# A list scheduler told other durations, and the Delta stage's projections in another order

## The chip, the core and the metric

The kernel runs on one core of one Trainium2 chip. Four engines do the work: TensorE (PE in the profile) multiplies, VectorE (DVE), ScalarE (ACT) and GpSimd (POOL) do the element-wise rest; SyncE (SP) issues most of the DMA. Each engine takes its instructions in the order in which the program lists them. The time is the device time of one execution in microseconds, the median of three runs. Before the change it is 1763.18 us (1761.16 to 1765.25).

## What is computed

512 tokens of width 1024 go through a block of two layers and then through a second block. A layer is a mixer and a gated feed-forward part, each with norms around it. The first layer's mixer is a dilated attention, the second layer's a gated delta rule in both directions ("Delta stage" here); both have an attention over a memory of 256 rows beside them. The mixer that the change touches, cut down:

```python
def _deltanet_sublayer(h, mem_n, w_in, conv_w, a_log, dt_bias, out_norm, w_out, w_mem_kv):
    qkv, z, gate_in, q_mem = jnp.split(h @ w_in, [...], axis=-1)
    qkv = lax.conv_general_dilated(qkv, conv_w[:, None, :], ...)
    q, k, v = jnp.split(jax.nn.silu(qkv), 3, axis=-1)       # six heads of 128
    q = _l2norm(q.reshape(b, s, DN_HEADS, DN_HEAD_DIM)) * (DN_HEAD_DIM ** -0.5)
    k = _l2norm(k.reshape(b, s, DN_HEADS, DN_HEAD_DIM))
    ...
    o = _gated_delta_chunked(q, k, v, ...) + rev(_gated_delta_chunked(rev(q), rev(k), ...))
    o = o * lax.rsqrt(jnp.mean(o * o, axis=-1, keepdims=True) + EPS) * out_norm * jax.nn.silu(zf)
    mem_out = _memory_attention(q_mem, mem_n, w_mem_kv)
    return jnp.concatenate([o, mem_out], axis=-1) @ w_out

def _gated_delta_chunked(q, k, v, g, beta):                  # chunks of 64 tokens
    ...
    sol = lax.linalg.triangular_solve(a, rhs, lower=True, unit_diagonal=True)
    u, w = sol[..., :dv], sol[..., dv:]
    def step(state, inp):
        v_new = uc - w @ state
        out = (q * exp(g)) @ state + intra @ v_new
        state = state * exp(g_last) + k.T @ v_new
        return state, out
```

The first block's second half, the norms and the second block's mixers are computed as well; the change leaves their arithmetic alone.

## The kernel before

**Precision.** A wide product is made of three matmuls: both operands are split into a high and a low part, and `mm3` (lines 271 to 273) issues low times high, high times low and high times high into one bank of PSUM. A weight arrives by DMA as `raw`, ScalarE writes its high part `wh` (line 243), VectorE or GpSimd its low part `wl` (line 262). A projection of 128 columns is eight such products of 128x512, over eight tiles of the width.

**Stages.** To about 75 us: norms of memory and tokens, the memory's keys and values, biases. To about 235 us: dilated attention and the memory's attention. To about 660: out-projection and feed-forward part of the first layer (`out_ffn`, line 1022). To about 1006: the Delta stage (`deltanet`, line 1170). To about 1430: its out-projection and the second feed-forward part. Then the second block, to 1756.

**What sets the order.** The whole program is laid out when the kernel is built, by a list scheduler, class `Flow`. Every piece of work is a generator that yields an engine and a stated duration and then emits its instructions; `run` (line 105 on) keeps a modelled time for each engine, and takes, of all pieces that are ready, the one that can start first in that model, with ties inside 0.1 us settled by a number `late`. A hand-over from one engine to another counts `HOP` = 0.2. The stated durations are those of `act`, `dve` and `pool` (lines 149 to 160) and the numbers in the yields: 0.33 for a product of 256 columns, 0.65 for one of 512. So a stated duration changes no instruction; it changes where each instruction stands in its engine's order, everywhere behind it.

**The Delta stage.** `deltanet_weights` (line 1161) gives the order in which the 27 projections of the stage run: `g` for the gates, four kinds `k`, `q`, `v`, `z` (`z` is the output gate) for each of six heads, and two `m`, the memory's queries. For each head, the triangular solve is an inverse by doubling: products `x` (lines 1519 and 1523), then `y` (1544), copies of `U` on VectorE (1548) and of `xT` on ScalarE (1530), at the end `y` (1566) and `Uf` (1571, on VectorE; 1558 on GpSimd). Then four steps of a chain, forward and backward side by side: product with `Uf` (1602), `vn` on ScalarE (1605), `vs` on VectorE (1610), product (1612), state `St` on VectorE (1616, 1619), product (1594), `rhs` on VectorE (1597), and again; the output `o` is made beside it (1624, 1625). `gate_out` (1645) then takes the head's row sums, the norm (GpSimd, 1352 and 1658), the transposition `poT` (1335) and the gate (1661); 1706 and 1708 split the result into `Xh` and `Xl` for the out-projection. The memory's attention (`mem_attention`, line 842) has the products `ms_s` (858), `ms_t` (882) and `mo` (898).

**What fills the waits.** Projections, products of the memory's attention and of other heads stand between the steps of a head. Once all projections are through, the out-projection of the stage may begin: `OUT[1]` (line 1727) lets a first group of three token tiles run over the tiles of the width in the order 6, 7, 0, 1, 2, 3, 4, 5, so that 21 products (those over the first seven) need nothing of the last head.

Of the kernel before, what the change touches and what calls it, by code (L numbers as in the profile page):

```python
# [35 lines left out]
S = 512  # L36
# [19 lines left out]
class Flow:  # L56
# [4 lines left out]


    HOP = 0.2

    def __init__(self, **sets):
        self.free = dict.fromkeys(("PE", "ACT", "DVE", "POOL", "DMA"), 0.0)
# [32 lines left out]
    def run(self):  # L99
        while self.threads:  # L100
            again = True
            while again:
                again = False
                for t in list(self.threads):
                    kind, *arg = t["req"]
                    value = None
                    if kind == "get" and any(self.sets[n] for n in arg):
                        value = min((n for n in arg if self.sets[n]), key=lambda n: min(self.sets[n])[0])
                        tok = min(self.sets[value])
                        self.sets[value].remove(tok)  # L110
                    elif kind == "two" and len(self.sets[arg[0]]) > 1:
                        for _ in range(2):
                            tok = min(self.sets[arg[0]])
                            self.sets[arg[0]].remove(tok)
                    elif kind == "wait" and all(e["tok"] for e in arg):
                        tok = max((e["tok"] for e in arg), key=lambda x: x[0])
                    elif kind == "move" and self.sets[arg[0]]:
                        src, dst = arg
                        tok = min(self.sets[src])
                        self.sets[src].remove(tok)  # L120
                        self.put(dst, tok)
                        tok = t["tok"]
                    elif kind == "late":
                        t["late"] = arg[0]
                        tok = t["tok"]
                    else:
                        continue
                    if tok[0] > t["tok"][0]:
                        t["tok"] = tok
                    self.step(t, value or tok)  # L130
                    again = True
            ops = []
            for t in self.threads:
                if t["req"][0] in self.free:
                    eng, cost, *after = t["req"]
                    ops.append((self.start(eng, after or [t["tok"]]), t))
            assert ops or not self.threads, ([(t["gen"].__name__, t["req"]) for t in self.threads], self.sets, self.free)
            if not ops:
                return
            s, t = min(ops, key=lambda x: x[0])  # L140
            s, t = min((x for x in ops if x[1]["req"][0] == t["req"][0] and x[0] <= s + DELTA), key=lambda x: x[1]["late"])
            eng, cost = t["req"][:2]
            self.free[eng] = s + cost
            t["tok"] = (s + cost, eng)
            self.step(t, t["tok"])
# [17 lines left out]
class K:  # L163
# [132 lines left out]
    def inputs(self, F, W, eX, eM, eF, pro):  # L296
# [93 lines left out]
        def memory():  # L390
            yield "late", 0.5
            for l in range(2):
                yield "wait", *eN[l]
                for c in range(2):
                    ev = W["mk"][l][c]
                    yield "wait", ev
                    yield "get", "mm"
                    p = self.psum("mm")
                    w = ev["W"]
                    for k in range(KT):  # L400
                        t = yield "PE", 0.33
                        self.mm3(p[:, :256], (w.h[:, k, :], w.l[:, k, :]), (M[l].h[:, k, :], M[l].l[:, k, :]),
                                 k == 0, k == KT - 1)
                    F.put("wsl", t)
                    F.add(evac(self.memK[l][:, c, :], p), 0.5, t)
                yield "wait", *W["mv"][l]
                for u in range(2):
                    yield "get", "mm"
                    p = self.psum("mm")
                    ts = slice(u * P, (u + 1) * P)  # L410
                    for k in range(KT):
                        w, kk = W["mv"][l][k // 4]["W"], k % 4
                        t = yield "PE", 0.33
                        self.mm3(p[:, :256], (M[l].h[:, k, ts], M[l].l[:, k, ts]), (w.h[:, kk, :], w.l[:, kk, :]),
                                 k == 0, k == KT - 1)
                    F.add(evac(self.memV[l][:, u, :], p, l == 1 and u == 1), 0.5, t)
                for _ in range(2):
                    F.put("wsl", t)
# [120 lines left out]
    def attention(self, F, W, eX, eM, eB, at, e2):  # L539
# [41 lines left out]
        def group(g):  # L581
# [37 lines left out]
            for i, t0 in enumerate((0, 64, 192, 320, 384)):  # L619
                yield "get", "mm"  # L620
                p = self.psum("mm")
                for k in range(KT):
                    w, kk = W2[k // 4]["W"], k % 4
                    t = yield "PE", 0.33
                    self.mm3(p[:, :256], (X.h[:, k, t0:t0 + P], X.l[:, k, t0:t0 + P]), (w.h[:, kk, :], w.l[:, kk, :]),
                             k == 0, k == KT - 1)
                F.add(copy_v(g, i, p[:, :256], r["t"][2][:, i, :], "mm"), g - 0.5, t)
# [394 lines left out]
    def out_ffn(self, F, i, W, gnext, groups, kev, before):  # L1022
# [57 lines left out]
        for part, (f0, f1) in enumerate(self.PARTS):  # L1080
# [22 lines left out]
            while f < nf:  # L1103
                fs = (f, f + 1) if part == 0 and f == 0 else (f,)
                banks = {}
                for hv in ((0, 256), (256, 512)) if len(fs) == 2 else ((0, 512),):
# [3 lines left out]
                    for f_ in fs:  # L1110
                        for z in range(2):
# [4 lines left out]
                                banks[f_, z] = self.psum("bk"), nm  # L1116
                            p = banks[f_, z][0]
                            for k in range(KT):
                                tk = yield "PE", 0.65 * (t1 - t0) / 512
                                self.mm3(p[:, t0:t1], (ev["W"].h[:, k, :], ev["W"].l[:, k, :]),  # L1120
                                         (X.h[:, k, t0:t1], X.l[:, k, t0:t1]), k == 0, k == KT - 1)
                            if t1 == S:
# [37 lines left out]
    def deltanet_weights(self):  # L1160
# [2 lines left out]
        r = {n: [self.weight(w, 0, KT, z * 768 + h * P, P) for h in range(6)] for z, n in enumerate("qkvz")}  # L1163
        r["g"] = self.weight(w, 0, KT, 3072, P)
        r["m"] = [self.weight(w, 0, KT, 3096 + c * P, P) for c in range(2)]
        N = 3
        heads = [[r[n][h] for n in ("kqvz" if h < N else "kqv")] for h in range(6)]
        return r, [r["g"]] + sum(heads[:3], []) + r["m"] + sum(heads[3:], []) + r["z"][N:]

    def deltanet(self, F, wev, order, eX, res):  # L1170

# [598 lines left out]
    def proj(self, F, ev, eX, m=P):  # L1770
# [7 lines left out]
        for t0, t1 in rngs:  # L1778
            yield "wait", *eX[t0 // P:t1 // P]
            for k in range(KT):  # L1780
                t = yield "PE", 0.65 * (t1 - t0) / S
                self.mm3(p[:m, t0:t1], (W.h[:, k, :], W.l[:, k, :]), (X.h[:, k, t0:t1], X.l[:, k, t0:t1]),
                         k == 0, k == KT - 1)
        F.put("wsl", t)
# [3 lines left out]
    def projector(self, F, items, eX, eP, late=20, haste=0):  # L1788
# [9 lines left out]
        def part(it, t0, t1):  # L1798
            W, m = it["W"], it["args"][4]
            yield "wait", *eX[t0 // P:t1 // P]  # L1800
            for k in range(KT):
                t = yield "PE", 0.65 * (t1 - t0) / S
                self.mm3(it["p"][:m, t0:t1], (W.h[:, k, :], W.l[:, k, :]), (X.h[:, k, t0:t1], X.l[:, k, t0:t1]),
                         k == 0, k == KT - 1)
            if t1 == S:
# [13 lines left out]
        for i, it in enumerate(items):  # L1819
# [13 lines left out]
            for u in range(4):  # L1833
# [3 lines left out]
                sl = slice(u * P, (u + 1) * P)  # L1837
                for k in range(KT):
                    W, kk = it[k // 4]["W"], k % 4
                    t = yield "PE", 0.33  # L1840
                    self.mm3(p[:, :256], (X.h[:, k, sl], X.l[:, k, sl]), (W.h[:, kk, :], W.l[:, kk, :]),
                             k == 0, k == KT - 1)
                evac, late_ = it[0]["use"]["f"]
# [392 lines left out]
    def s5(self, F, W, eX, open_, eY, uT):  # L2236
# [140 lines left out]
        def glu():  # L2377
# [14 lines left out]
            for c in range(2):  # L2392
                zs = []
                for o in (2, 0):
# [1 line left out]
                    p = self.psum("lv", "glu")  # L2396
                    os_ = slice((o + c) * P, (o + c + 1) * P)
                    for k in range(2):
                        t = yield "PE", 0.65
                        self.mm3(p, (w.h[:, k, os_], w.l[:, k, os_]), yh[k], k == 0, k == 1)  # L2400
                    zs.append((p, t))
                if c:
# [896 lines left out]
```

## Time and profile before

| | |
|---|---|
| median of three runs | 1763.18 us (1761.16 to 1765.25) |
| the profiled execution | 1761.48 us, span 1759.5 us, mean granted clock 0.993 |
| TensorE busy | 1708.7 us, 97% |
| VectorE, ScalarE, GpSimd busy | 979.8 us (56%), 763.2 us (43%), 338.0 us (19%) |
| share of the chain that ended last | TensorE 84%, VectorE 9%, ScalarE 2% |

Busy time is counted in the trace of one execution. A matmul's row shows its start and a modelled length; since matmuls overlap, the distance between two starts tells more than the length. An "idle before" in brackets is time in which the engine had nothing to run, with what ended it. The granted clock of TensorE is 1 at 2.4 GHz and 0.5 at 1.2 GHz; a mean between these says that a stretch had both.

### The profile page before, as it was taken

The numbers are of one execution on the slowest core, as the hardware profiler recorded it, in microseconds if no ns is written. First come the engines' busy times: TensorE is split into PE (matmuls) and PEld (weight loads), VectorE is DVE, ScalarE is ACT, GpSimd is POOL, SyncE is SP. The second block draws the span as 40 slices with busy tenths as digits, with TensorE's granted clock in tenths as the row PEclk, the third lists the DMA queues.
The fourth block names the chain that finished last, engine by engine and source line by source line (L and its number), as shares of the span: only waits on it lengthen the run. The fifth ranks groups of instructions, "written<-read, shape, count | busy, mean of one in ns | idle before, by whom it ended". The sixth has DMA issues, their size and how long they took to land.

```text
span 1759.5 us, 30190 instructions
## 1 busy us (share of the span) xinstructions
PE 1708.7 (97%) x12031; PEld 1423.2 (81%) x12031; DVE 979.8 (56%) x1997; ACT 763.2 (43%) x1808; POOL 338.0 (19%) x496
## 2 busy tenths in 40 slices
PE   6999999999999999999999899999999999999999
PEld 5988679888888888788777788888888888888787
DVE  6333656323333378867887467464433468467573
ACT  5443635333223245656555355333223353345671
POOL 5200001000000021220222351364540033210000
PEclk9999999999999999999999999999999999999999
DMA  6513133333233332211110164345333253552012
GB/s 195 154 51 95 49 120 97 120 96 96 96 96 96 96 114 79 61 38 38 38 37 32 59 152 139 109 133 144 108 108 96 77 159 115 153 154 69 25 37 84
DMA packets 211981, 167.84 MB, mean 95 GB/s; under 512 B 21996, under 2 KB 183036, under 8 KB 211840
## 3 DMA queue, kind: packets, MB, share of 16 engines
q1 hardware_dynamic: 203808, 154.39, 29.7%
q0 software_dynamic: 4560, 9.42, 2.1%
q10 hardware_dynamic: 3472, 2.10, 0.4%
q8 instruction: 94, 1.54, 0.4%
q14 instruction: 47, 0.39, 0.1%
HBM read 152.23 MB, written 13.65 MB: 94 GB/s over the span
## 4 chain that ended last, share of the span: by engine, by line
PE 84%; DVE 9%; ACT 2%; issue 2%; DMA 1%; POOL 1%; ACTq 0%; SPq 0%; DVEq 0%; POOLq 0%
PE bk L271 23%; PE bk L272 22%; PE bk L273 22%; DVE hn L1324 2%; DVE wl L262 1%; PE no L2753 1%; PE npT L2736 1%; PE x L1519 1%; PE x L1523 1%; PE y L1544 1%; DVE hs L942 1%; PE ns L2722 1%; PE hT L949 1%; PE ns L2720 1%; PE o L1625 1%
## 5 line engine op out<-in xcount | busy, mean ns | idle before, releaser
L262 DVE TENSOR_TENSOR wl<-raw,wh 128x512 fp32r<-128x512 f32 x450 | 315.8, 742 | 372.4 <-ACT wh L243 371.8
L243 ACT ACTIVATE wh<-raw 128x512 fp32r<-128x512 f32 x474 | 273.0, 623 | 534.4 <-PE bk L273 300.4
L271 PE MATMUL bk<-Xh,wl 128*128 128x512 f32 (+2 forms) x1312 | 494.9, 377 | 0.2 <-ACT Xh L951 0.2
L272 PE MATMUL bk<-Xl,wh 128*128 128x512 f32 (+2 forms) x1312 | 478.4, 365 | 0.5 <-DVE Xl L956 0.5
L273 PE MATMUL bk<-Xh,wh 128*128 128x512 f32 (+2 forms) x1312 | 478.5, 365 | 0.0
L273 PEld LDWEIGHTS bk<-Xh,wh 128*128 128x128 f32 (+1 forms) x1312 | 246.9, 188 | 40.1
L271 PEld LDWEIGHTS bk<-Xh,wl 128*128 128x128 f32 (+1 forms) x1312 | 247.5, 189 | 39.0 <-issue 3.5
L272 PEld LDWEIGHTS bk<-Xl,wh 128*128 128x128 f32 (+1 forms) x1312 | 247.7, 189 | 34.8 <-DVE Xl L956 0.9
L271 PE MATMUL bk<-wh,Xl 128*128 128x512 f32 (+1 forms) x424 | 152.6, 360 | 6.7 <-DVE Xl L796 3.7
L272 PE MATMUL bk<-wl,Xh 128*128 128x512 f32 (+1 forms) x424 | 145.8, 344 | 0.3 <-DVE wl L262 0.2
L273 PE MATMUL bk<-wh,Xh 128*128 128x512 f32 (+1 forms) x424 | 145.2, 342 | 0.0
L271 PE MATMUL bk<-wh,Al 128*128 128x512 f32 x352 | 139.7, 397 | 0.0
L272 PE MATMUL bk<-wl,Ah 128*128 128x512 f32 x352 | 139.5, 396 | 0.0
L921 POOL TENSOR_TENSOR nc<-ncm,nhalf 128x1 f32<-128x1 f32 x16 | 11.5, 720 | 661.9 <-DVE ncm L919 661.9
L273 PE MATMUL bk<-wh,Ah 128*128 128x512 f32 x352 | 138.6, 394 | 0.0
L1093 DVE TENSOR_TENSOR sg<-sg,bk 128x512 f32<-128x512 f32 x44 | 30.2, 687 | 124.7 <-PE bk L273 120.2
L271 PEld LDWEIGHTS bk<-wh,Xl 128*128 128x128 f32 x424 | 84.7, 200 | 18.0 <-DVE Xl L796 3.1
L273 PEld LDWEIGHTS bk<-wh,Xh 128*128 128x128 f32 x424 | 84.8, 200 | 8.1
L272 PEld LDWEIGHTS bk<-wl,Xh 128*128 128x128 f32 x424 | 85.0, 200 | 7.6 <-DVE wl L262 1.0
L271 PEld LDWEIGHTS bk<-wh,Al 128*128 128x128 f32 x352 | 66.0, 188 | 16.1
L273 PEld LDWEIGHTS bk<-wh,Ah 128*128 128x128 f32 x352 | 66.0, 188 | 16.0
L272 PEld LDWEIGHTS bk<-wl,Ah 128*128 128x128 f32 x352 | 66.1, 188 | 15.4
(586 smaller groups left out, 2623.8 us busy)
## 6 DMA issues: line engine op xcount, KB each, us to landing
raw<-in_ffn_w_gate_up_dram SPq DMA_DIRECT2D x88, 512.0 KB, 3.9
raw<-in_ffn_w_down_dram SPq DMA_DIRECT2D x44, 512.0 KB, 3.3
raw<-in_dn_w_in_dram SPq DMA_DIRECT2D x27, 512.0 KB, 4.0
raw<-in_att_w_in_dram SPq DMA_DIRECT2D x20, 512.0 KB, 4.1
raw<-in_w_in_dram SPq DMA_DIRECT2D x20, 512.0 KB, 3.8
raw<-in_mem_w_kv_dram SPq DMA_DIRECT2D x8, 512.0 KB, 3.6
raw<-in_att_w_out_dram SPq DMA_DIRECT2D x8, 512.0 KB, 3.3
xd<-x SPq DMA_DIRECT2D x8, 512.0 KB, 2.6
```

Source lines behind the costliest of these rows:

```text
L243: nc.scalar.activation(wh[:, sl], ev["raw"][:, sl], AF.Copy)
L262: eng.tensor_tensor(wl[:, sl], raw[:, sl], wh[:, sl].bitcast(F32), op=OP.subtract)
L271: mm(out, A[1], B[0], start=first, stop=False, **kw)
L272: mm(out, A[0], B[1], start=False, stop=False, **kw)
L273: mm(out, A[0], B[0], start=False, stop=last, **kw)
L942: nc.vector.scalar_tensor_tensor(hh[:, hv[i]], x[:, t, hv[i]], r2, r["gain"][:, hv[i]], op0=OP.mult, op1=OP.mult)
L949: nc.tensor.transpose(p[:, k * P:(k + 1) * P], hh[:, i * 512 + k * P:i * 512 + (k + 1) * P], self.ident)
L1093: nc.vector.tensor_tensor(sg, sg, pu, op=OP.mult)
L1324: nc.vector.scalar_tensor_tensor(acc[:, d0:d1], raw[:, d0 + o:d1 + o], cw[:, ti, tap:tap + 1], acc[:, d0:d1], op0=OP.mult, op1=OP.add)
L1519: nc.tensor.matmul(dn8(b[i])[at], lhsT, rhs, start=True, stop=True)
L1523: nc.tensor.transpose(b[d][:, o:o + P], U[:, d, 2 * n:2 * n + 2, :].rearrange("p c q -> p (c q)"), self.ident)
L1544: nc.tensor.matmul(dn8(ys[par])[HB[f], d, n, :], T[d][HB[par], n, f, :], xs[f][HB[par], d, n, :], start=True, stop=True)
```

## The change

Three edits. The scheduler adds 0.08 us to every stated duration on VectorE and 0.07 on ScalarE. The stated durations of TensorE's wide products become 0.36 for 0.33 and 0.682 for 0.65. The projections of the Delta stage get a written order: the keys of the next head come before a head's `z`, and the two `m` before the fourth head's `q`.

```diff
+    STEP = {"DVE": 0.08, "ACT": 0.07}
...
             eng, cost = t["req"][:2]
+            cost += self.STEP.get(eng, 0.0)
             self.free[eng] = s + cost
...
-                        t = yield "PE", 0.33
+                        t = yield "PE", 0.36
...
-                                tk = yield "PE", 0.65 * (t1 - t0) / 512
+                                tk = yield "PE", 0.682 * (t1 - t0) / 512
...
-        N = 3
-        heads = [[r[n][h] for n in ("kqvz" if h < N else "kqv")] for h in range(6)]
-        return r, [r["g"]] + sum(heads[:3], []) + r["m"] + sum(heads[3:], []) + r["z"][N:]
+
+        k, q, v, z = (r[n] for n in "kqvz")
+        order = [r["g"], k[0], q[0], v[0]]
+        for h in (1, 2, 3):
+            order += [k[h], z[h - 1]] + (r["m"] if h == 3 else []) + [q[h], v[h]]
+        return r, order + [k[4], q[4], v[4], k[5], q[5], v[5], z[3], z[4], z[5]]
```

The 0.33 stands in four places (memory's keys and values, the attention's values, the projector's narrow items), the 0.65 in four (gate and up products of the feed-forward part, both ways of a projection, the second block's `glu`). The projections' order before is g, then k q v z of heads 0 to 2, m m, k q v of heads 3 to 5, z of heads 3 to 5; after it is g, k0 q0 v0, k1 z0 q1 v1, k2 z1 q2 v2, k3 z2 m m q3 v3, k4 q4 v4, k5 q5 v5, z3 z4 z5. Line numbers of the changed kernel are two higher than before up to 1160, and five higher behind the new list.

The order that results differs in all stages. Three places on TensorE follow; `bk` is a bank of PSUM, `wh,Xl` and the like are the parts of a wide product.

TensorE at the start of the last head's chain, before:

```order
L1602 MATMUL chain<-vtok,Uf 128x128 x2
L271 MATMUL bk<-wh,Xl 128x512
L272 MATMUL bk<-wl,Xh 128x512
L273 MATMUL bk<-wh,Xh 128x512
L1612 MATMUL chain<-vs_9650,ktok 128x128
L1612 MATMUL chain<-vs_9653,ktok 128x128
L1625 MATMUL o<-vn_9643,AT_8938 128x128
L271 MATMUL bk<-wh,Xl 128x512
L272 MATMUL bk<-wl,Xh 128x512
L273 MATMUL bk<-wh,Xh 128x512
L1594 MATMUL chain<-St_9657,kTh 128x128
L1625 MATMUL o<-vn_9648,AT_9055 128x128
```

A wide product of the out-projection stands ahead of each step. The same place after:

```order
L1571 MATMUL y_9681<-xT_9676 64x64
L1607 MATMUL chain<-vtok,Uf 128x128 x2
L1617 MATMUL chain<-vs_9703,ktok 128x128
L1617 MATMUL chain<-vs_9705,ktok 128x128
L1630 MATMUL o<-vn_9699,AT_8999 128x128
L1630 MATMUL o<-vn_9701,AT_9148 128x128
L1599 MATMUL chain<-St_9709,kTh 128x128
L1599 MATMUL chain<-St_9713,kTh 128x128
L1607 MATMUL chain<-rhs_9721,Uf 128x128
L1607 MATMUL chain<-rhs_9723,Uf 128x128
L1617 MATMUL chain<-vs_9731,ktok 128x128
L1617 MATMUL chain<-vs_9733,ktok 128x128
```

There the chain's steps and the outputs `o` follow each other; the out-projection's products that stood between them have moved ahead of the head's last inverse step, all but one of the 21. The five products that stood between the last `o` and `poT` have moved there too.

TensorE in the chain of the third head, before:

```order
L1594 MATMUL chain<-St_7910,kTh 128x128
L1602 MATMUL chain<-rhs_7915,Uf 128x128
L1335 MATMUL pv<-ident,vTh 128x128 x4
L1602 MATMUL chain<-rhs_7948,Uf 128x128
L271 MATMUL bk<-Xh,wl 128x512
L272 MATMUL bk<-Xl,wh 128x512
L273 MATMUL bk<-Xh,wh 128x512
L1612 MATMUL chain<-vs_7964,ktok 128x128
L1544 MATMUL y_7973<-xT_7944 64x64
```

One projection product stands ahead of the step at line 1612. After:

```order
L1549 MATMUL y_7961<-xT_7938 64x64
L1607 MATMUL chain<-rhs_7958,Uf 128x128
L1607 MATMUL chain<-rhs_7981,Uf 128x128
L1340 MATMUL pv<-ident,vTh 128x128 x4
L860 MATMUL ms_s<-memK_75,oT 128x256 x4
L273 MATMUL bk<-Xh,wl 128x512
L274 MATMUL bk<-Xl,wh 128x512
L275 MATMUL bk<-Xh,wh 128x512
L1617 MATMUL chain<-vs_8007,ktok 128x128
L1617 MATMUL chain<-vs_8012,ktok 128x128
```

Now both directions' products with `Uf` come together, and `pv`, the memory's `ms_s` and a projection product stand ahead of the pair with `vs`.

TensorE at the end of the dilated attention, behind the last projection, before (`atp`, `ao`, `as` belong to the band attention, `fbc` to its normalisation):

```order
L898 MATMUL mo<-mpT,memV_99 64x128 x8
L858 MATMUL ms_s<-memK_98,oT 128x256 x4
L687 MATMUL atp<-ident,sb 128x128 x8
L706 MATMUL ao<-pT,V_882 64x128 x8
L658 MATMUL as<-kT_1281,qT_1280 128x128 x4
L882 MATMUL ms_t<-ident,mp 128x128 x8
L898 MATMUL mo<-mpT,memV_99 64x128 x8
L764 MATMUL fbc<-ident,amx 64x128 x12
L658 MATMUL as<-kT_1281,qT_1280 128x128 x4
L271 MATMUL bk<-wh,Xl 128x512
L272 MATMUL bk<-wl,Xh 128x512
```

Two groups `ms_t`, `mo` of the memory's attention stand behind the last projection, and the first out-projection product follows soon after the second. After:

```order
L884 MATMUL ms_t<-ident,mp 128x128 x8
L900 MATMUL mo<-mpT,memV_99 64x128 x8
L708 MATMUL ao<-pT,V_845 64x128 x4
L766 MATMUL fbc<-ident,amx 64x128 x6
L860 MATMUL ms_s<-memK_98,oT 128x256 x4
L766 MATMUL fbc<-ident,amx 64x128 x6
L689 MATMUL atp<-ident,sb 128x128 x4
L766 MATMUL fbc<-ident,amx 64x128 x6
L708 MATMUL ao<-pT,V_845 64x128 x4
L660 MATMUL as<-kT_1285,qT_1284 128x128 x4
L884 MATMUL ms_t<-ident,mp 128x128 x8
L900 MATMUL mo<-mpT,memV_99 64x128 x8
```

A third group, with its own `ms_s`, stands ahead of the first out-projection product.

## Rows read from the trace of the kernel before

**Rows 1.** The page's busy line and the shares of the chain that ended last.
```profile
PE 1708.7 (97%) x12031; PEld 1423.2 (81%) x12031; DVE 979.8 (56%) x1997; ACT 763.2 (43%) x1808; POOL 338.0 (19%) x496
PE 84%; DVE 9%; ACT 2%; issue 2%; DMA 1%; POOL 1%; ACTq 0%; SPq 0%; DVEq 0%; POOLq 0%
```

**Rows 2.** Windows: busy us (count) of PE, PEld, DVE, ACT, POOL; clock; DMA.
```profile
203.00:219.00 16.00, 12.50 (x132) 9.09 (x132) 14.34 (x40) 11.14 (x42) 0.00 (x0) 1.00 0.11 35
220.00:240.00 20.00, 16.88 (x132) 13.16 (x133) 13.46 (x30) 7.02 (x19) 0.00 (x0) 0.91 0.09 28
660.00:700.00 40.00, 36.51 (x227) 32.19 (x226) 32.15 (x72) 23.23 (x56) 4.64 (x3) 0.96 0.31 85
700.00:860.00 160.00, 157.53 (x1922) 127.67 (x1922) 124.49 (x290) 96.95 (x263) 33.88 (x28) 1.00 0.16 44
860.00:880.00 20.00, 17.85 (x274) 15.05 (x273) 14.09 (x34) 9.62 (x33) 4.72 (x5) 0.91 0.10 28
940.00:960.00 20.00, 17.94 (x192) 15.36 (x191) 17.80 (x35) 8.21 (x28) 6.48 (x6) 0.91 0.08 28
1000.00:1020.00 20.00, 16.71 (x67) 12.87 (x65) 8.53 (x15) 8.29 (x22) 14.22 (x21) 0.91 0.68 179
```

**Rows 3.** Waits of PE, 662 to 978 us: total us, times, longest us.
```profile
PE chain L1612 <- DVE vs L1610: 5.3, 5, 1.4
PE pk L1335 <- DVE kraw L1305: 3.5, 2, 3.3
PE x L1519 <- DVE U L1506: 1.4, 1, 1.4
PE y L1544 <- ACT xT L1530: 1.1, 2, 0.9
PE chain L1602 <- DVE rhs L1597: 0.9, 1, 0.9
```

**Rows 4.** Timeline of PE, the last head's chain: start us, us, line, idle before.
```profile
981.66 0.47 PE L1566 MATMUL y<-xT 64*64 64x64 f32 x16
...
983.56 0.60 PE L1602 MATMUL chain<-vtok,Uf 128*128 128x128 f32 x4
983.92 0.48 PE L271 MATMUL bk<-wh,Xl 128*128 128x512 f32 x1
984.24 0.40 PE L272 MATMUL bk<-wl,Xh 128*128 128x512 f32 x1
984.70 0.64 PE L1612 MATMUL chain<-vs,ktok 128*128 128x128 f32 x4
...
986.11 0.38 PE L1594 MATMUL chain<-St,kTh 128*128 128x128 f32 x2
...
998.65 0.39 PE L1625 MATMUL o<-vn,AT 128*128 128x128 f32 x2
...
1003.40 0.66 PE L1335 MATMUL poT<-ident,otok 128*128 128x128 f32 x4 [0.92 <-POOL otok L1658]
1006.28 0.50 PE L271 MATMUL bk<-wh,Xl 128*128 128x512 f32 x1 [2.23 <-DVE Xl L1708]
```

**Rows 5.** Timeline of DVE in the same stretch.
```profile
984.29 0.51 DVE L1610 TENSOR_SCALAR vs<-vn,ksc 128x128 f32<-128x128 f32 x2
...
986.53 0.35 DVE L1597 SCALAR_TENSOR_TENSOR rhs<-chain,neg,vtok 128x128 f32<-128x128 f32 x1 [0.26 <-PE chain L1594]
```

**Rows 6.** Waits of PE, 978 to 1007 us.
```profile
PE bk L271 <- DVE Xl L1708: 2.9, 2, 2.2
PE poT L1335 <- POOL otok L1658: 0.9, 1, 0.9
```

**Rows 7.** Timeline of PE: one row of the front, two of the attention's end.
```profile
30.37 1.07 PE L354 MATMUL hT<-ident,hs 128*128 128x128 f32 x8 [2.34 <-DVE hs L346]
...
215.13 1.09 PE L898 MATMUL mo<-mpT,memV 128*64 128x128 f32 x16 [1.03 <-DVE mpT L888]
...
234.86 0.50 PE L271 MATMUL bk<-wh,Xl 128*128 128x512 f32 x1 [2.84 <-DVE Xl L796]
```

More of the change, by code (lines that the diff above doesn't have):

```diff
@@ L412, in memory @@
                         w, kk = W["mv"][l][k // 4]["W"], k % 4
-                        t = yield "PE", 0.33
+                        t = yield "PE", 0.36
                         self.mm3(p[:, :256], (M[l].h[:, k, ts], M[l].l[:, k, ts]), (w.h[:, kk, :], w.l[:, kk, :]),
@@ L623, in group @@
                     w, kk = W2[k // 4]["W"], k % 4
-                    t = yield "PE", 0.33
+                    t = yield "PE", 0.36
                     self.mm3(p[:, :256], (X.h[:, k, t0:t0 + P], X.l[:, k, t0:t0 + P]), (w.h[:, kk, :], w.l[:, kk, :]),
@@ L1780, in proj @@
             for k in range(KT):
-                t = yield "PE", 0.65 * (t1 - t0) / S
+                t = yield "PE", 0.682 * (t1 - t0) / S
                 self.mm3(p[:m, t0:t1], (W.h[:, k, :], W.l[:, k, :]), (X.h[:, k, t0:t1], X.l[:, k, t0:t1]),
@@ L1801, in part @@
             for k in range(KT):
-                t = yield "PE", 0.65 * (t1 - t0) / S
+                t = yield "PE", 0.682 * (t1 - t0) / S
                 self.mm3(it["p"][:m, t0:t1], (W.h[:, k, :], W.l[:, k, :]), (X.h[:, k, t0:t1], X.l[:, k, t0:t1]),
@@ L1839, in projector @@
                     W, kk = it[k // 4]["W"], k % 4
-                    t = yield "PE", 0.33
+                    t = yield "PE", 0.36
                     self.mm3(p[:, :256], (X.h[:, k, sl], X.l[:, k, sl]), (W.h[:, kk, :], W.l[:, kk, :]),
@@ L2398, in glu @@
                     for k in range(2):
-                        t = yield "PE", 0.65
+                        t = yield "PE", 0.682
                         self.mm3(p, (w.h[:, k, os_], w.l[:, k, os_]), yh[k], k == 0, k == 1)
```

## The prediction

> **What bounds the kernel now.** I read the page's busy line first, then the chain that ended last. TensorE is busy 97% of the span and 84% of the last chain is TensorE [rows 1]; VectorE and ScalarE stand at 56% and 43%. The multiset of products is the same before and after, so time can come only from the holes in TensorE's row, from stretches at the lower clock, and from how its products join. The whole span has some 50 us of holes. The reader should then take the windows [rows 2]: from 700 to 860 us TensorE stands still for 2.5 us of 160, but 860 to 880, 940 to 960 and 1000 to 1020 each lose 2 to 3.3 us and show a granted clock of 0.91. A mean of 0.91 over 20 us is 0.09 x 20 / 0.5 = 3.6 us at 1.2 instead of 2.4 GHz, so some 1.8 us lost each time; 220 to 240 and 660 to 700 hold one such drop each. These stretches are the Delta stage (about 662 to 1006 us) and the end of the attention stage. The waits of TensorE in 662 to 978 us [rows 3] say what it waits for: 5.3 us for VectorE's `vs` in five places, 3.5 for the first keys, the rest small. With two of 0.4 that are not quoted they add up to 13.0 us; the 3.5 are the first key's, 1.1 belong to the last head's inverse, which leaves 8.4 us in the middle of the stage.
>
> **The end of the Delta stage, the largest term.** The order on TensorE after the change takes the projections earlier, and so also the out-projection products (lines 271 to 273 with `wh,Xl` first) that may run before the last head's output is there. There are 21 of these. Before, all 21 lie in the last head's own work, from the end of its inverse to the transposition `poT` at 1003.40 [rows 4]: one or two between each two steps of its chain, and five behind the last `o`. After, 20 of the 21 stand ahead of the last head's last inverse step, and from its first chain product to `poT` nothing stands between the steps. What that costs comes from [rows 4, 5]:
> - The last inverse product starts at 981.66 and the first chain product at 983.56, because `Uf` goes through VectorE: 1.90 us, of which the inverse's own products take 0.45. Two products (0.32 + 2 x 0.23 = 0.78 us each, starts of 983.92, 984.24 and half the way to 984.70) filled this; unfilled it is a wait of 1.45 us.
> - A chain step hands over to ScalarE and VectorE for `vs`: first chain product 983.56, `vs` from 984.29, two of them in 0.51, so the next product could start at about 984.6: 1.07 after the first, less 0.44 for a pair, is 0.65. For `rhs`: 986.11, `rhs` from 986.53 for 0.35, so 0.8 less 0.44, about 0.4. Four waits for `vs` and three for `rhs` make 2.6 + 1.2 = 3.8 us; the state `St` is covered by the two `o` pairs, which still stand there.
> - From the last `o` at 998.65 to the next out-projection product at 1006.28 it is 7.6 us of row sums, norm on GpSimd, transposition and split. Of it 0.9 us are `o` and `poT`. Before, five products filled 3.6 of it and 0.92 + 2.23 = 3.15 us were waits; after, 6.7.
> - One product instead of two stands between the last inverse steps: 0.3.
>
> The last head thus waits 1.45 + 3.8 + 6.7 + 0.3 = 12.3 us. The head before it starts its chain unfilled too, since there the projections have just run out: 1.0 for its last inverse step (between 0 and the 1.56 us that two products covered in the last head before), 1.45 for `Uf` and 0.65 for `vs`, 3.1 us. Together 15.4, against 4.9 us before (1.1 for `xT` [rows 3], 2.9 for splits and 0.9 for `otok` [rows 6]). So **+10.5 us**, bounded below by +7.5 (head 4's start is free, chain waits at 0.4 each) and above by +14 (the chain is no shorter than the 15.1 us it took before, though 11 products at 0.78, 8.6 us, have left it).
>
> **The middle of the Delta stage.** The same products now stand between the steps of earlier heads: in the place shown, a score product of the memory's attention beside a projection, where before a projection stood alone; the least fill between two inverse steps is larger too. VectorE's cost in the planner rises by 0.08 us per operation, so a `vs` behind others in VectorE's queue is no longer promised too early. Of the 8.4 us I leave 1.5, as in the 160 us from 700, which held 2.5: **-6.9 us** (ends: -8.4 and -4). The wait for the first keys stays, since g, k0, q0 and v0 lead in both orders.
>
> **The clock.** Two drops lie in the middle, behind waits for `vs`, and would go with them: -3.6 us. But head 4's start and the last head's start each get over 2 us of waits close together, which is what preceded the drops at 683 (3.3 us [rows 3]) and 1006 us, so I put two drops there: +3.6. Sum 0, ends -3.6 and +1.8.
>
> **The attention's end.** One block more of the memory's attention stands behind the last projection. Its hand-overs cost TensorE 1.03 us for `mpT` where nothing covered it [rows 7]; two such make **+2.1 us** until the steady out-projection starts, which was at 234.86. Ends: -1 (the band attention beside it covers it) and +4 (with a drop of the clock).
>
> **The front.** The tokens' tiles are loaded together ahead of the memory's weights and the transposition that waited 2.34 us at 30.37 [rows 7] comes earlier, with fewer memory products ahead of it. I take **+0.5**, ends -1 and +3.
>
> **Joins and the rest.** A product of three matmuls in a run of its kind takes 0.23 us a matmul; the first matmul of a run takes 0.32 to the next start [rows 4]. The order has 302 such runs instead of 321: 19 x 0.09 = **-1.7 us**. Four loads of ScalarE's tables fall away, on an engine that is busy 43% of the span and that only 1.1 us of the waits above name: nothing. The stated costs of TensorE's products (0.36 for 0.33, 0.682 for 0.65) issue nothing; they act through the order only. The remaining stages, the feed-forward parts and the second block, are as before but for small exchanges: 0, ends -1.5 and +1.5.
>
> **Sum:** 10.5 - 6.9 + 0 + 2.1 + 0.5 - 1.7 = +4.5 us. The profiled execution took 1761.48 us (span 1759.5), which would become 1766.0. It lies 1.7 us below the median, near the fastest of the three runs, so I add the sum to the median: 1763.18 + 4.5 = 1767.7, **1768 us**.
>
> **The rivals.**
> - Faster. Waits in the middle and both of their drops of the clock go (-8.4 - 3.6), the tail costs its lower bound (+7.5), attention and front are neutral, joins -1.7: -6.2, so 1757. For it: VectorE, on which the middle waits, is at 78% from 700 to 860 us [rows 2], so a truer price for its operations bears exactly there. Against it: the tail's hand-overs can be counted one by one and nothing stands in them. Chance 0.24.
> - No change. The sum as above, but the two drops do not come back in the tail: 4.5 - 3.6 = +0.9, so 1764. The work that fills is only moved, and holes before and behind are paid alike. Chance 0.22. That the change does nothing to the order is no case of its own; the order differs in every stage.
> - Slower still. In the last head's chain the clock falls for the whole of it. Its products are 15.1 - 8.6 = 6.5 us of work; at the lower clock that is 6.5 more, of which part falls into the 3.8 us of waits, so about +4 on the sum: 1772. It decides if waits of half a microsecond, one after another, are enough. From 203 to 219 us TensorE was busy 12.5 of 16 us, with the wait of 1.03 [rows 7] among others, and the clock stayed at 2.4 GHz [rows 2]; the unfilled chain would be busy 6.5 of 10.3, less than that. The Trainium skill (TensorE: Matmul & The Clock Gate, A second HAM failure mode: psum-queue depth-cycling) says that short idle times between groups of matmuls, if frequent, make the clock swing between its levels; by that rule this case would hold. The stretch at 203 us does not agree with it. Chance 0.12.
> - The forecast itself, 1762 to 1772 about 1768: 0.42.
>
> **How the numbers follow.** A measurement can tell about 0.2%, 3.5 us, from no change: below 1759.7 is faster, above 1766.7 slower. The faster rival gives 0.22 faster and 0.02 same; no change gives 0.17 same, 0.03 faster and 0.02 slower; the forecast 0.36 slower and 0.06 same; the clock's case 0.12 slower. That is 0.25, 0.25 and 0.50. The range takes in most of the faster rival and the clock's: 1756 to 1776. Without the faster rival it would be 1762 to 1774.
>
> **What would show it.** In the trace of the changed kernel: waits of `bk` for `Xl` and of `poT` for `otok` near the stage's end that add up to 6 to 7 us (2.9 + 0.9 before); six or seven waits of 0.3 to 0.7 us in the last head's chain; waits of TensorE for `vs` in the middle under 2 us together; two clock drops near 970 to 990 us instead of those in the windows at 860 and 940. The out-projection of the attention should start steadily near 237 us. I am wrong if the middle still waits several microseconds (then it is slower than forecast), or if the last head's chain ends earlier by more than its missing products, so that the stage ends before 1006 us.

## The result: slower by 1.4%, and where the time went

The changed kernel takes 1789.73 us in the median of four runs (1784.6 to 1790.38), the kernel before 1763.59 in the four runs beside it (1761.16 to 1765.25). The ratio is 1.0143, with a 95% interval of 1.0121 to 1.0165: slower by some 26 us, where 4.5 were forecast and the range ended at 1776. The direction was right and the size was not.

The profiled execution is the fastest of the four, 1784.6 us with a span of 1782.9, so the trace explains 23.4 us against the span of 1759.5 before. The page's busy line and shares of the last chain, which answer to [rows 1]:

```profile
PE 1710.7 (96%) x12031; PEld 1425.2 (80%) x12031; DVE 971.8 (55%) x1997; ACT 758.9 (43%) x1804; POOL 340.0 (19%) x496
...
PE 86%; DVE 7%; ACT 2%; POOL 1%; issue 1%; DMA 1%; ACTq 0%; SPq 0%; DVEq 0%; POOLq 0%
```

TensorE is busy 2.0 us longer with the same 12031 matmuls, so 21.4 of the 23.4 us are holes. I summed TensorE's idle times over 0.08 us in its timeline, stage by stage, before and after:

| stage | before | after | difference |
|---|---|---|---|
| front, to 100 us | 14.5 | 14.3 | -0.2 |
| attention's end, 200 to 240 | 6.8 | 9.7 | +2.9 |
| first feed-forward part | 0.4 | 3.0 | +2.6 |
| its end, to the Delta stage | 2.4 | 2.3 | -0.1 |
| Delta stage, start, to 702 | 3.3 | 6.7 | +3.4 |
| Delta stage, middle, to 952 | 8.6 | 4.5 | -4.1 |
| Delta stage, last two heads, to the first product that needs the last one | 4.9 | 13.7 | +8.8 |
| second out-projection and feed-forward part | 0.9 | 3.6 | +2.7 |
| its end, to the second block | 2.8 | 3.3 | +0.5 |
| second block | 1.9 | 7.0 | +5.1 |

The differences add up to 21.6. With the 2.0 us of busy time this is the span's difference to within 0.2.

Windows of the changed kernel by stage (length, then busy time and count of PE, PEld, DVE, ACT and POOL, the granted clock, DMA share, GB/s) answer to [rows 2]:

```profile
200.00:240.00 40.00, 30.23 (x296) 23.11 (x297) 31.27 (x76) 22.13 (x74) 0.00 (x0) 1.00 0.09 27
...
665.00:705.00 40.00, 33.25 (x209) 29.70 (x208) 30.04 (x73) 21.70 (x54) 3.26 (x3) 0.91 0.30 80
705.00:860.00 155.00, 153.86 (x1832) 124.38 (x1832) 119.61 (x271) 92.35 (x246) 32.19 (x27) 1.00 0.17 46
860.00:880.00 20.00, 19.16 (x225) 16.43 (x224) 17.59 (x38) 12.04 (x36) 5.45 (x4) 1.00 0.11 28
...
940.00:1025.00 85.00, 71.32 (x865) 57.33 (x864) 43.89 (x112) 33.37 (x93) 23.52 (x27) 0.90 0.12 32
1025.00:1065.00 40.00, 36.43 (x182) 30.13 (x181) 27.52 (x54) 21.29 (x48) 22.61 (x40) 0.96 0.55 133
...
1450.00:1783.00 333.00, 322.04 (x2733) 268.26 (x2732) 198.19 (x440) 158.69 (x409) 40.13 (x44) 1.00 0.33 93
```

From 705 to 880 us TensorE is now all but gapless and its clock stays up: that is the gain that was meant. The line of 940 to 1025 is the price, 13.7 us idle in 85. A clock of 0.91 over 40 us and 0.90 over 85 mean 7.2 + 17 us at 1.2 GHz there, where the Delta stage of before had 3.2 + 3.6 + 3.6 + 3.6 = 14 us [rows 2]. Head 4's start and the gap behind the last `o` show where the 17 lie:

```profile
955.00:970.00 15.00, 10.91 (x94) 8.96 (x93) 12.96 (x25) 6.07 (x16) 5.10 (x5) 0.77 0.11 36
...
1012.00:1025.00 13.00, 6.67 (x19) 5.13 (x20) 3.47 (x8) 3.97 (x15) 10.63 (x15) 0.61 0.45 114
```

That is 6.9 and 10.1 us at 1.2 GHz, but in the second TensorE works for only 6.7 of 13 us, and where it stands still there is no product to lengthen. I laid the stretches at 1.2 GHz over TensorE's busy time in both whole traces: they hold 26.3 us of work, and 23.5 before, at half the clock some 1.4 us more lost. The drop in the attention's end is gone.

Waits of TensorE in the changed kernel (total us, times, longest us), first from 665 to 955 us, which answers to [rows 3]:

```profile
PE pk L1340 <- DVE kraw L1310: 4.8, 1, 4.8
PE chain L1607 <- DVE rhs L1602: 3.0, 3, 2.2
PE y L1508 <- DVE Ln L1427: 1.9, 1, 1.9
PE chain L1617 <- DVE vs L1615: 1.5, 3, 0.7
```

The five waits for `vs`, 5.3 us, are down to three, 1.5. But the first keys cost 4.8 instead of 3.3 (the 3.5 of [rows 3] are two waits; the other, 0.2, is for a later head's keys), and a single wait for `rhs` 2.2. Then from 955 to 1020 us, which answers to [rows 6]:

```profile
PE poT L1340 <- POOL otok L1663: 4.4, 1, 4.4
PE chain L1617 <- DVE vs L1615: 2.9, 5, 1.1
PE chain L1607 <- DVE Uf L1576: 2.9, 4, 1.5
PE bk L273 <- DVE Xl L1713: 2.2, 1, 2.2
PE chain L1607 <- DVE rhs L1602: 0.7, 3, 0.2
PE y L1571 <- ACT xT L1535: 0.6, 1, 0.6
```

This is the unfilled end as the order had shown it: no hand-over is missing from the list of the prediction. The timeline of TensorE in the last head's chain answers to [rows 4]:

```profile
999.12 0.46 PE L1607 MATMUL chain<-vtok,Uf 128*128 128x128 f32 x2 [0.46 <-DVE Uf L1576]
...
1002.80 0.75 PE L1607 MATMUL chain<-rhs,Uf 128*128 128x128 f32 x4 [0.22 <-DVE rhs L1602]
1004.04 0.74 PE L1617 MATMUL chain<-vs,ktok 128*128 128x128 f32 x4 [0.49 <-DVE vs L1615]
...
1016.10 1.12 PE L1340 MATMUL poT<-ident,otok 128*128 128x128 f32 x4 [4.36 <-POOL otok L1663]
1019.44 0.80 PE L273 MATMUL bk<-wh,Xl 128*128 128x512 f32 x1 [2.23 <-DVE Xl L1713]
```

What the prediction had put at nothing stands outside the Delta stage. Waits of the second block, before (1440 to 1760 us):

```profile
PE gs L2108 <- POOL ge L2087: 0.6, 1, 0.6
PE ncs L2663 <- DVE Q L2631: 0.5, 1, 0.5
PE npT L2736 <- ACT nP L2728: 0.3, 1, 0.3
```

and after (1455 to 1783 us):

```profile
PE gs L2113 <- POOL ge L2092: 1.6, 1, 1.6
PE ncsT L2679 <- ACT sqt L2673: 1.3, 1, 1.3
PE glu L273 <- DVE wl L264: 1.0, 1, 1.0
PE ns L2725 <- DVE Q L2636: 0.8, 1, 0.8
PE nkT L2592 <- DVE nkd L2587: 0.8, 1, 0.8
```

Mostly other products wait, and each a little longer: 1.9 us have become 7.0. In the second feed-forward part it is above all one place, the transposition of the third token tile's normed values:

```profile
1054.34 0.40 PE L275 MATMUL bk<-wh,Xh 128*128 128x512 f32 x1
1057.40 1.55 PE L951 MATMUL hT<-ident,hs 128*128 128x128 f32 x8 [2.66 <-DVE hs L944]
1058.60 0.56 PE L273 MATMUL bk<-Xh,wl 128*128 128x256 f32 x1
```

The first gate and up product (`Xh,wl`, 256 columns) now stands behind this transposition; before, such products of earlier tokens stood ahead of it, and the wait for `hs` there was 0.5 us in all.

The three other executions took 1789.6 to 1790.4 us at a mean granted clock of 0.986 to 0.989, where the profiled one had 0.990. A clock lower by 0.003 over 1785 us is at most 5.4 us, and the distance between them is some 5; where their drops lie no trace shows.

### The profile page after: what moved, and what is told of

It reads as the page before. It is cut to its first block, busy times and chain, and to the rows that moved or that the text cites. A ratio compares the mean times of both kernels' runs of the same rounds, so it can differ in the third digit from the quotient of the medians.

```text
span 1782.9 us, 30198 instructions
## 1 busy us (share of the span) xinstructions
PE 1710.7 (96%) x12031; PEld 1425.2 (80%) x12031; DVE 971.8 (55%) x1997; ACT 758.9 (43%) x1804; POOL 340.0 (19%) x496
## 4 chain that ended last, share of the span: by engine, by line
PE 86%; DVE 7%; ACT 2%; POOL 1%; issue 1%; DMA 1%; ACTq 0%; SPq 0%; DVEq 0%; POOLq 0%
PE bk L273 23%; PE bk L274 22%; PE bk L275 22%; DVE wl L264 1%; PE no L2758 1%; PE x L1524 1%; PE npT L2741 1%; PE x L1528 1%; PE y L1549 1%; DVE x L927 1%; PE ns L2727 1%; DVE hs L944 1%; POOL wl L264 1%; PE ns L2725 1%; PE chain L1607 1%
## 5 line engine op out<-in xcount | busy, mean ns | idle before, releaser
L923 POOL TENSOR_TENSOR nc<-ncm,nhalf 128x1 f32<-128x1 f32 x16 | 11.2, 698 | 657.7 <-DVE ncm L921 652.9
```

## The experiments

Three theories stood at first. A: an unfilled end of the Delta stage costs some 12 us whoever causes it, the durations the rest. B: the order of the projections is the loss. C: the durations are.

### One edit at a time

**Only the new order of the projections** (`e_order`): the new list of `deltanet_weights`, nothing else.

```diff
-        return r, [r["g"]] + sum(heads[:3], []) + r["m"] + sum(heads[3:], []) + r["z"][N:]
+        return r, order + [k[4], q[4], v[4], k[5], q[5], v[5], z[3], z[4], z[5]]
```

> Only the new order of the projections; all stated durations as before. Its last head's chain has no product between its steps (0 of 21), as in the changed kernel, while everything up to the Delta stage is as before. Theory A (an unfilled end of the Delta stage costs some 9 us of waits and 3 us of clock whoever causes it; the rest of the loss comes from the stated durations in the other stages): about 1775 us. Theory B (the order alone is the loss): about 1788. Theory C (the durations alone are the loss, the order is neutral): 1762 to 1766.

Measured: 1766.13 us, ratio 1.0016 (1.0006 to 1.0025). Its last chain is as empty as the changed kernel's. Waits of TensorE from 955 to 1030 us:

```profile
PE poT L1338 <- POOL otok L1661: 4.4, 1, 4.4
PE bk L271 <- DVE Xl L1711: 2.2, 1, 2.2
PE bk L271 <- ACT wh L243: 2.0, 1, 2.0
PE chain L1615 <- DVE vs L1613: 1.3, 3, 0.5
PE chain L1605 <- DVE rhs L1600: 0.7, 3, 0.2
```

The idle times of its last two heads up to 1024 us sum to 11.2 us against 5.3 before, those of its start and middle to 9.7 against 11.9. So the end costs some 6 us, of which 1.9 are a longer wait for a weight's high part (`wh`), the middle gives 2 back, and the clock is no worse, for 3 us in all. Head 4's start, where the changed kernel waits 4.1 us, waits only 0.5 here: that part of the end does not come with the order alone. Theory A's 12 us for the end are wrong by a factor of four on balance, and B falls.

**Only VectorE's and ScalarE's durations** (`e_step`):

```diff
+    STEP = {"DVE": 0.08, "ACT": 0.07}
...
+            cost += self.STEP.get(eng, 0.0)
```

> Only the 0.08 and 0.07 us added to VectorE's and ScalarE's stated durations; projections and TensorE's durations as before. Its last head's chain is unfilled too, and every stage is laid out anew. Theory A: 12 us for the end of the Delta stage and about 11 for the other stages, 1786. Theory B: 1762 to 1766. Theory C: 1786 to 1790.

Measured: 1795.36 us, ratio 1.0177 (1.0162 to 1.0193), no less than the whole change.

**Only TensorE's durations** (`e_pe`):

```diff
-                        t = yield "PE", 0.33
+                        t = yield "PE", 0.36
...
-                t = yield "PE", 0.65 * (t1 - t0) / S
+                t = yield "PE", 0.682 * (t1 - t0) / S
```

> Only TensorE's stated durations (0.36 and 0.682). The last head's chain keeps its 11 products, the five behind its last output are gone. Theory A: 3.5 us for those five and up to 3 of others, 1764 to 1770. Theory B: as before, 1762 to 1766. Theory C leaves open which of the durations does it: 1764 if VectorE's and ScalarE's do, up to 1788 if TensorE's do.

Measured: 1781.96 us, ratio 1.0102 (1.0082 to 1.0123). The last chain kept its products; most of the new holes are in the second block, 11.1 us against 1.9, and 3.4 more stand ahead of `poT`. Its waits from 1450 us on:

```profile
PE gs L2108 <- POOL ge L2087: 3.0, 2, 2.4
PE ncs L2663 <- DVE Q L2631: 2.3, 1, 2.3
PE nqT L2623 <- DVE nqd L2618: 2.0, 1, 2.0
```

**Everything but the order** (`e_step_pe`): the changed kernel with the old list.

> The changed kernel with the old order of the projections. The last head's chain is unfilled. Theory A: near the changed kernel, 1784 to 1790. Theory B: 1762 to 1766. Theory C: 1788.

Measured: 1790.14 us, ratio 1.0144 (1.0122 to 1.0165), the same as the changed kernel within the intervals. Theory C holds: the stated durations are the loss, and the new order of the projections costs 3 us alone and nothing that can be measured beside them.

### Where: the plan of one stage at a time

The durations were switched while the program is laid out: on only for the Delta stage, with the new order (`s_delta`), or on everywhere else, with the old order (`s_rest`). The switch goes back when the stage's last projection has been laid out and the out-projection may begin, so what is left of the last heads then, the last chain among it, is laid out with the durations of the other stages.

```diff
+    PE = {0.33: 0.36, 0.65: 0.682, 0.325: 0.341}
...
+            if self.on:
+                cost = self.PE.get(cost, cost) if eng == "PE" else cost + self.STEP.get(eng, 0.0)
...
+                F.on = not F.on
                 eK, eP, close = self.deltanet(F, W1, order1, eX, res)
                 yield "wait", eP, eK[6]
+                F.on = not F.on
```

> The new durations hold only while the Delta stage is planned, with the new order of the projections; the plan of all other stages goes by the old durations. If the loss adds up over the stages as the waits in the changed kernel's trace do (Delta stage: 8.7 us of waits and some 4 of clock), about 1775 us. If the Delta stage is the whole loss: 1788. If the loss is wholly elsewhere: 1762 to 1766.

Measured: 1771.16 us, ratio 1.0045 (1.0030 to 1.0060), so +8.6 us.

> The reverse: the new durations everywhere but in the plan of the Delta stage, which keeps the old durations and the old order. By the waits of the changed kernel's trace outside that stage (attention's end 2.9, the two feed-forward parts 2.6 and 2.7, the second block 5.6 with its entry) about 1777. If the Delta stage is the whole loss: 1762 to 1766. If any new layout costs the whole again: 1788.

Measured: 1781.83 us, ratio 1.0112 (1.0097 to 1.0127), so +19.2 us. Together 27.8, against the change's 26: the stages add up within the intervals. Its window of the second block lacks 10.1 us of 329:

```profile
1450.00:1779.00 329.00, 318.89 (x2688) 264.67 (x2686) 196.70 (x438) 157.54 (x406) 39.97 (x44) 0.99 0.33 94
```

The changed kernel has 11.0 of 333 there; in both some 4 are the output after the last product. Not all of the 19.2 lies outside the Delta stage, though. By their sources, `s_rest` has 16.8 us of holes more than the kernel before: 10.5 in the feed-forward parts and the second block, 2.5 in the front and the attention's end, none in the Delta stage's start and middle, and 3.7 in its last heads, where the gap ahead of `poT` has grown from 0.9 us:

```profile
PE poT L1340 <- POOL otok L1663: 3.7, 1, 3.7
```

So about half of the loss lies where the prediction had put zero.

### Is the empty end a loss of its own?

In `t_hold` the changed kernel's out-projection waits until the last head's inverse is done, so that its products fill the last chain; `t_order_hold` does the same to the order alone.

```diff
             r["eU"]["tok"] = max(t, tP)
+            if h == 5:
+                self.eU5["tok"] = r["eU"]["tok"]
...
-                yield "wait", eP, eK[6]
+                yield "wait", eP, eK[6], self.eU5
```

> The changed kernel, but the out-projection of the Delta stage is held back until the last head's inverse is done, so that its 20 products fill the last chain again (12) and the gap behind the last output (8). If the empty end is a loss of its own, as forecast: 8 to 10 us less than the changed kernel, 1780. If fill is only moved, since head 4's chain and the last inverse now go without: 1786 to 1792.

Measured: 1792.7 us, ratio 1.0176 (1.0154 to 1.0199): 3 us more than the changed kernel, which the intervals do not tell from none, and not 8 to 10 less. Waits of TensorE from 955 to 1030 us and a window of the same stretch:

```profile
PE chain L1609 <- DVE Uf L1576: 2.6, 4, 1.5
PE x L1524 <- DVE U L1553: 2.5, 4, 0.9
PE chain L1619 <- DVE vs L1617: 2.0, 3, 1.1
PE bk L273 <- DVE Xl L1715: 1.5, 1, 1.5
PE y L1549 <- ACT xT L1535: 1.5, 5, 0.5
```

```profile
955.00:1030.00 75.00, 63.80 (x683) 52.22 (x682) 35.95 (x95) 25.61 (x73) 19.51 (x22) 0.84 0.06 16
```

The gap ahead of `poT` is closed, and the last inverse, now without products, waits 4 us for `U` and `xT` instead. The clock is 0.84 in this stretch, 24 of 75 us at 1.2 GHz. Holding back has a second price, from 1030 to 1050 us:

```profile
PE bk L273 <- ACT wh L245: 4.1, 1, 4.1
```

ScalarE, which makes `wh`, waits there 6.7 us for the DMA of the out-projection's next weight (`raw`); the changed kernel lost 0.4 us at this place.

> Only the new order of the projections, old durations, and the out-projection held back in the same way (11 products in the last chain, 8 behind the last output). If the empty end is a loss of its own: 7 us less than the order alone, 1759. If fill is only moved: 1765 to 1770.

Measured: 1772.49 us, ratio 1.0057 (1.0040 to 1.0074), 6 us more than the order alone, with the same wait for a weight, 4.4 us against 2.0, and some 20 us at 1.2 GHz from 969 us on. In both the holes from head 4's start to the split fall by only some 2.5 us, and the wait for the weight takes that back: fill is moved, not made.

### How sensitive is the plan to its numbers?

Two theories of the durations. S: size and sign matter, longer numbers for TensorE put too little under each wait. R: the order before is a favourable one among many, and any other numbers lay the program out worse. In the diffs only the numbers differ from those above: 0.331 and 0.652 (`p_pe_tiny`), 0.30 and 0.618 (`p_pe_down`), 0.01 for both engines (`p_step_tiny`), -0.03 for both (`p_step_down`).

> The kernel before with TensorE's stated durations moved by 0.3% (0.331 for 0.33, 0.652 for 0.65), which says nothing new of the machine. Theory S (size and sign: longer stated durations of TensorE put too little under each wait, and the loss grows with them, 19 us at +9% and +5%): 1763 to 1765. Theory R (the order before is a favourable outcome among many; any other set of numbers lays the program out anew and loses some 10 to 30 us whatever its size or sign): 1772 to 1785.

Measured: 1767.18 us, ratio 1.0022 (1.0010 to 1.0034). For 0.3% in the numbers (0.001 and 0.002 us, less than a row of the timeline can show), the five products behind the last output have gone elsewhere, and the wait ahead of `poT` is 4.4 us instead of 0.9. Its waits from 975 to 1012 us:

```profile
PE poT L1335 <- POOL otok L1658: 4.4, 1, 4.4
PE bk L271 <- DVE Xl L1708: 2.2, 1, 2.2
```

> TensorE's stated durations moved as far as in the change but the other way (0.30 for 0.33, 0.618 for 0.65). Theory S: more work under each wait than the plan believes, so no slower than before in the stages behind the front, 1755 to 1766. Theory R: 1772 to 1790.

Measured: 1771.7 us, ratio 1.0057 (1.0040 to 1.0073), with 8.7 us of holes in the second block.

> 0.01 us instead of 0.08 and 0.07 added to VectorE's and ScalarE's stated durations. Theory S: an eighth of the 32 us, 1764 to 1768. Theory R: 1772 to 1795.

Measured: 1772.85 us, ratio 1.0062 (1.0047 to 1.0077).

> 0.03 us taken from each stated duration of VectorE and ScalarE. The last head's chain keeps 8 products and 7 behind its last output. Theory S: no loss by overstated durations, 1755 to 1768. Theory R: 1772 to 1795, with the waits spread over the stages.

Measured: 1772.1 us, ratio 1.0052 (1.0037 to 1.0067); it keeps the filled end, and has among others a wait of 3.2 us for a weight's high part at the start of the out-projection.

Neither theory stands whole. S fails on the signs: the opposite moves cost 9 us each too. R fails in the smallest move, 4 us, and meets the other three only at the lower edge of its ranges: they cost 9 to 10 us, none of them the 19 or 32 of the large ones upward.

### Which of the durations?

Last, the additions on short operations alone (`k_small`: stated under 0.4 us) or on long ones alone (`k_big`), and TensorE's two numbers apart (`k_pe256`: 0.36, `k_pe512`: 0.682).

```diff
+            if cost < 0.4:
+                cost += self.STEP.get(eng, 0.0)
```

> The additions of 0.08 and 0.07 us only on VectorE's and ScalarE's operations with a stated duration under 0.4 us (the small ones of norms and chains). Theory L (the addition on long operations makes the weights' conversions look dearer than they are, so they are planned late and TensorE runs out of products): 1765 to 1772. Theory M (small operations carry it, since there are more of them in every chain): 1785 to 1795.

Measured: 1788.98 us, ratio 1.0152 (1.0122 to 1.0182).

> The additions only on operations with a stated duration of 0.4 us or more (the 512-wide ones: conversions, splits, evictions). Theory L: most of the 32 us, 1782 to 1795, with the wait of 2.7 us for the third norm tile of the second feed-forward part. Theory M: 1765 to 1772.

Measured: 1801.28 us, ratio 1.0217 (1.0201 to 1.0232), the slowest of all.

> Only 0.36 for 0.33 (256-column products: memory's keys and values, values of the attention, narrow projections of the second block). If the 19 us of TensorE's durations come from the plan of the second block, where these stand: 1770 to 1780. If from the wide products: 1762 to 1767.

Measured: 1768.36 us, ratio 1.0038 (1.0018 to 1.0057).

> Only 0.682 for 0.65 (512-column products: projections, gate and up products). If these carry the 19 us: 1775 to 1785, with the Delta stage's last gap as in the run with both. If the 256-column ones do: 1764 to 1770.

Measured: 1770.45 us, ratio 1.0041 (1.0026 to 1.0056).

The additions on either half of the operations cost 25 to 38 us, on both 32. TensorE's two numbers cost 5 to 7 us each and 19 together, and 11.1 us of holes in the second block with both stand against 6.9 and 6.0 with one; given the intervals these may add up. Theories L and M both fall: on VectorE and ScalarE the loss is not the sum of what its parts cost (25 and 38, together 32), nor is it between them and TensorE (32 and 19, together 27).

## Why the prediction was right in its direction and wrong in its size

- **End of the Delta stage** (forecast +10.5): +8.8 us of holes. The gap behind the last `o` was 6.7 by forecast and 4.36 + 2.23 = 6.6 measured; the chain's waits 3.8 and 2.1, since pairs of `rhs` cost 0.22, not 0.4, and of `vs` 0.49, not 0.65; the first `Uf` 1.45 and 0.9; head 4's start 3.1 and 4.1. The step held.
- **Middle** (-6.9): the waits for `vs` did go, 5.3 to 1.5 us, but the first keys wait 1.5 us more, `Ln` at 700 us takes 1.9 and one `rhs` 2.2. Start and middle together gain 0.7 us. The step failed where it took the wait for the first keys to stay, and the least fill between steps for the fill at each. The prediction's own sign of being wrong, a middle that still waits several microseconds, came true: 4.5 us, and 6.7 before 702.
- **Clock** (0, ends -3.6 and +1.8) and **joins** (-1.7): the two drops of the middle went, and head 4's start and the gap behind the last `o` got 17 us at 1.2 GHz instead. Head 4's start drew a drop as forecast; the last head's start did not; the second drop came in the gap instead, where little work lay. The clock cost 1.4 us, inside its ends. TensorE's busy time rose by 2.0, so 0.6 remain for all else: the 1.7 us of joins did not come out of it, and no run takes them apart.
- **Attention's end** (+2.1): +2.9, and the steady out-projection starts at 237.3, where 237 was forecast. **Front** (+0.5): -0.2. Both held.
- **"The remaining stages ... are as before but for small exchanges: 0, ends -1.5 and +1.5"**: this is the step that failed. The first feed-forward part lost 2.6 us, the second 2.7, the second block 5.1, with the entries 10.8 in all; the run with the new durations everywhere but in most of the Delta stage's plan confirms it with 10.5 us of holes in these stages. I had read the order there for its large features and found none; in the second feed-forward part the gate and up products no longer lie over a hand-over; for the second block the waits are shown, and not what moved. From profile to profile the miss is 23.4 - 4.5 = 18.9 us: 10.8 here, 6.2 in the middle, 3.7 in clock and joins, less 1.7 at the end.
- **The rivals.** That the clock falls in the last chain did not happen: from 996 to 1012 us TensorE was busy 12.7 of 16 us in waits of 0.2 to 0.5 and stayed at 2.4 GHz:

```profile
996.00:1012.00 16.00, 12.73 (x109) 10.16 (x108) 7.46 (x26) 4.03 (x14) 1.88 (x2) 1.00 0.02 7
```

With only VectorE's and ScalarE's durations changed, the same chain did lose clock, but there the last inverse ahead of it had waited 1.6 us too (997 to 1001), where the changed kernel has no wait:

```profile
1000.00:1016.00 16.00, 12.80 (x95) 10.77 (x90) 7.18 (x25) 4.17 (x14) 1.84 (x2) 0.89 0.00 1
```

The Trainium skill (TensorE: Matmul & The Clock Gate, A second HAM failure mode: psum-queue depth-cycling) has short idle times make the clock swing if they are frequent; the first of these two rows does not agree with it, the second does. The rival "no change", in which work that fills is only moved, fits what the order alone did, where the middle gave back a third of what the end cost; that its 1764 lies near the 1766 of that run is luck, since its sum was made for all three edits.
- **The direction.** It does not hang on the failed step alone: the Delta stage by itself has +8.1 us of holes, where 10.5 - 6.9 = 3.6 were forecast.

**What stays open.** That the stated durations are the cause is shown, and in which stages, up to where the switch went back. Why numbers nearer to the trace give a worse order is not. Nearer they are for the commonest operations: in the trace before, a split into `wl` takes 0.742 us on VectorE (stated 0.608, then 0.688), one into `wh` 0.624 on ScalarE (0.53, then 0.60), a product of 512 columns 3 x 0.23 = 0.69 (0.65, then 0.682). Of the sixteen other orders that were run, none was faster than before; they lie between +0.16% and +2.2%, and the smallest change of a number is among the nearest. That fits an order before which the old numbers happen to serve well, but no run sorts out which decision of the plan turns a number into a wait. No version beat the kernel before.

## What to carry to other kernels

When a change touches the durations by which a scheduler lays out a whole program, cost every stage of the program, not the one that the change is named for: here 13.5 of 21.6 us of new holes lay outside it, in single hand-overs. Run a change of no meaning (here 0.3% in TensorE's numbers, 4 us) beside it before believing that a truer number is a better one. And where work fills waits, moving it pays at one end and costs at the other; in four layouts that place the same 21 products elsewhere none was better than the one before.

## What had not been expected of the hardware

The three unprofiled runs of the changed kernel were 5 us slower than the profiled one at the same order of instructions. The mean clock (0.986, 0.987 and 0.989 against 0.990) would make up to 7.1, 5.4 and 1.8 us of it, so it accounts for the distance in two of the three. TensorE's busy time for the same matmuls was 1708.7 us before, 1710.7 in the changed kernel, 1717.9 with the additions on VectorE and ScalarE alone, and 1725.7 in the changed kernel with the out-projection held back. Two windows of the last beside the one above:

```profile
200.00:245.00 45.00, 35.79 (x303) 27.69 (x302) 31.51 (x76) 22.48 (x74) 0.00 (x0) 0.89 0.07 24
...
1030.00:1100.00 70.00, 62.96 (x362) 54.86 (x361) 42.37 (x90) 32.56 (x72) 35.63 (x62) 0.93 0.56 140
```

Its idle times sum to 67.2 us, less than the changed kernel's 68.1, and yet its profiled execution, the slowest of its four, ended 14 us later, with 15.0 us more of busy time. Its stretches at 1.2 GHz hold 48.4 us of work against 26.3, which is 11 of the 15; what the other 4 are is not shown.
